# A hybrid encoder layer on one core: another order of three dense products, before and inside retention

## The chip, the core and the metric

The kernel runs on one core of a Trainium2 chip. A core has a matrix engine (TensorE, PE in the profile, whose weight loads are listed as PEld), a vector engine (VectorE, DVE), an activation engine (ScalarE, ACT), a general engine (GpSimd, POOL) and SyncE (SP), which here issues nearly all DMAs. Each engine works through its own queue of instructions in order. TensorE writes its results to the memory PSUM; here ScalarE or VectorE copies them out ("evicts" them), and a PSUM buffer is used again only after that. The metric is device time in microseconds (us) of one execution, as a median over runs.

## What is computed

One encoder layer is applied to a prompt of 1024 rows and a sample of 256 rows with the same weights, which the kernel handles as 1280 tokens, ten blocks of 128. Cut to what matters:

```python
proj = rms_norm(h, norm_g) @ w_in
(a_qkv, a_gate, a_beta, a_alpha, b_q, b_k, b_v, b_gate, c_q, c_k, c_v, c_gate) = split(proj)
# a: gated delta rule, forward and backward, 6 heads of 64
o_a = rms_norm(delta(q, k, v, beta, g) + flip(delta(flipped))) * silu(a_gate)
# b: retention, forward and backward, 6 heads of 64
o_b = head_layer_norm(retention(bq, bk, bv) + flip(retention(flipped))) * silu(b_gate)
# c: windowed attention with sink and ALiBi, 4 query heads, 2 key heads
o_c = window_attention(cq, ck, cv, sink) * silu(c_gate)
h = h + concat(o_a, o_b, o_c) @ w_out
h = h + (p @ w_ple) * sigmoid(h @ w_pg)
return rms_norm(h, final_g)
```

Inside a chunk of 64 tokens the delta rule needs the inverse of a triangular 64 x 64 matrix; between chunks a 64 x 64 state is passed on. All numbers are 32-bit floats.

## The kernel before

**Dense products.** The projection is cut into products of 128 columns for all 1280 tokens. For near-full precision each 32-bit operand is split into a high and a low part, and a product is the sum of three matmuls (high-high, low-high, high-low) over eight slices of the inner dimension. `dense` runs over token blocks of 512, 512 and 256; each block is 24 matmuls into one PSUM buffer with the tag `mm`, which has two. So two finished blocks can wait for their eviction, and a third cannot start. The weights of the next product are loaded (`raw`) and split (`whi`, `wlo`) one product ahead by `dense_stream`.

The products have short names. Numbers are gates: 0, 1 and 2 are the gates of the delta rule's three pairs of heads, 3 to 5 those of retention's three pairs, 6 and 7 those of attention. `cq0`, `cq1`, `ck`, `cv` are attention's queries, keys and values. `q0` to `q2`, `k0` to `k2`, `v0` to `v2` are retention's, one for each pair of heads. In the order rows and the trace they all read `mm<-xh,whi`; a number behind `mm` is one block, a number behind `whi` one product.

**Evictions.** A `q`, `k` or `v` is evicted by one ScalarE copy per block (L390). A gate takes a copy to `sz` (L468), three activations that make a sigmoid in `sg` (L100 to L102), a VectorE product (L89), and for gates 0 to 5 a DMA to DRAM (`gd`, L472). `sz` and `sg` have one buffer each. Gates 0 to 2 are read back only at the kernel's end, in `fin`; gates 3 to 5 in `av`.

**Where they go.** The region `ot` has eight slots of 1280 columns. k0 and k2 are evicted into slot 0 and every `v` into slot 1; k1 goes to a tile of its own, `kx`. Slots 0 and 1 are also where the triangular inverses are built: `invert` (from L398 on) is a chain of some sixty VectorE operations on these slots, run for two groups of chunks, one after the other. Its end is a memset (L424) and two stores to DRAM (`yd`, L426). The first eviction of k0 must wait until the second group's stores have read slot 0.

**Streams.** Three streams run at once. The *scan* (`scan_stream`) joins the inverses into full ones (`join`: `an`, `yn`, `p1s`, `yc`, tiles in PSUM tag `sb`) and then takes twenty steps forward and backward (`step`: small matmuls into `sa`, state copies `sv` at L729 and L730, the residual `r`, loads of `l`, `yc`, `vt`, `kn`). The *fill* (`fill`) runs attention over ten blocks, with the products of the list `PB` beside it, then retention. For each of the three pairs retention first does `kv(p)` (transposes at L942 and L947, `sb<-bvt,kd`, and a chain of state sums on VectorE at L966) and then `av(p)` (scores `ss`, output, norm). The list `RS` says which products stand beside each of these seven places. The first chain of sums for pair p reads slot 1, so the eviction of the next `v` waits for it.

**What sets the order.** `spread` and `weave` interleave the streams as the program is written, by weights such as `T_AT` and `T_KV`. The framework's scheduler then orders each engine's instructions by an estimate of its own, with evictions at high priority. So two lists of names decide the order only through that scheduler. The rows shown below are what it makes of them.

Of the kernel before, what the change touches and what calls it, by code (L numbers as in the profile page):

```python
# [34 lines left out]
AO = tuple(range(NB))  # L35
X2, SPN = 4, 0
PP = ["cq0", "cq1", 6, 7, 3, "ck", "cv", 4, 0, 5]
PB = [1, 2, "q0"]
RS = [["k0", "v0"], ["q1"], ["k1", "v1"], ["k2"], ["v2"], ["q2"], []]
T_PREP = 10.0  # L40
YB, VB, KB, QB = 1, 2, 1, 1
QLB = 1
# [11 lines left out]
def encoder_kernel(ctx: ExitStack, tc: tile.TileContext, I, O, dbg=None, upto=99):  # L54
# [385 lines left out]
    def spread(*run):  # L440

        run = [[0.0, t, g] for t, g in run]
        while run:
            q = min(run, key=lambda e: e[0])
            t = next(q[2], None)
            if t is None:
                run.remove(q)
            else:
                q[0] += t / q[1]
                yield t  # L450

    def length(ns):
        return 12.8 * len(ns) or 1.0, prods(*ns)
# [31 lines left out]

    PSEQ = PP + PB + [n for r in RS for n in r]

    def prods(*names):
        for n in names:
            i = PSEQ.index(n)  # L490
            yield from dense_stream(n, PSEQ[i + 1] if i + 1 < len(PSEQ) else None)
# [588 lines left out]
    def fill():  # L1080
        nonlocal av
        yield from spread((10 * T_AT, attn_stream()), length(PB))
        cb_cm.__exit__(None, None, None)
        rc_cm, rt_cm, *r = ret_open()
        kv, av = ret_streams(*r)
        yield from prods(*RS[0])
        for p in range(3):
            yield from spread((13 * T_KV, kv(p)), length(RS[1 + 2 * p]))
            if p < 2:
                yield from spread((5 * T_AV, av(p)), length(RS[2 + 2 * p]))  # L1090

        raw = [a[:, 0:4 * GW].rearrange("p (k c) -> p k c", k=4) for a in (kreg[1], ot[:, 1, :])]
        for i in range(2):
            nc.sync.dma_start(out=raw[i], in_=I["w_out"][0][512 * i:512 * i + 512, 0:GW].rearrange("(k p) c -> p k c", p=128))
        yield from spread((5 * T_AV, av(2)), length(RS[6]))

# [120 lines left out]
```

## Time and profile before

| | |
|---|---|
| median of 3 runs | 1095.5 us (1093.81 to 1100.48) |
| the profiled execution | 1098.55 us |
| its span, first to last instruction | 1096.7 us |
| mean granted TensorE clock | 0.959 |
| attention (first scores to the last output) | about 350 to 598 us |
| second inversion ends on VectorE | 463.45 us |
| retention's three pairs of keys start at | 598.8, about 702 and 776.1 us |

Times in the trace count from the span's start. In the rows of the timeline a line gives the start, the duration, the engine, the source line, the operation, what it writes and reads, the shapes and the count; a bracket at its end gives the idle time of that engine before it and what ended it. In a row of windows the stretch is followed by its length and by the busy time of PE, PEld, VectorE, ScalarE and GpSimd, each with a count, then the granted TensorE clock, the share of DMA time and GB/s. A row of the chain of waits has a start, a duration and what the end of the program was waiting for. Matmul rows overlap, because matmuls are pipelined: the pace is the distance of their starts. A matmul of two 32-bit operands that are not split shows as two in the trace (12 for a row of 6 in the order).

### The profile page before, as it was taken

Reading aid. Unit: us, or ns where it says so; the run is one execution under the profiler, and the core shown is the slowest. Engines: PE = TensorE matmul, PEld = TensorE weight load, DVE = VectorE, ACT = ScalarE, POOL = GpSimd, SP = SyncE. Lnnn points to the kernel's source line nnn. Section 1 sums busy time; section 2 is a strip of 40 time slices with the busy share of each in tenths; the row PEclk is TensorE's granted clock in tenths of the full one; section 3 lists DMA queues with packets and bytes.
Section 4 is the critical chain, followed back from the end, with each engine's and each line's share of the span. In section 5 each row is a group of like instructions: output and inputs, shape, how many; then the busy total and the mean of one; then the engine's idle time right before and its main releaser. Section 6 shows DMA issues by size and latency. Waiting matters only on the chain.

```text
span 1096.7 us, 23201 instructions
## 1 busy us (share of the span) xinstructions
PE 1023.4 (93%) x8909; PEld 868.3 (79%) x8909; DVE 640.9 (58%) x1371; ACT 521.8 (48%) x1265; POOL 271.3 (25%) x430
## 2 busy tenths in 40 slices
PE   5999999999897889999998899999799999999996
PEld 4768878887775767878776777777579999999996
DVE  6666677477799679845565755575883123311125
ACT  7576776577456445344444322323342013455554
POOL 2001000022123021222233325544442211233421
PEclk9999999999999889999999799969889999999999
DMA  8112112367866363463464334554372432101003
GB/s 259 35 44 68 44 39 61 75 169 199 194 176 186 84 159 86 111 136 86 111 167 120 108 92 122 138 152 115 112 244 86 144 112 78 39 1 49 11 39 154
DMA packets 201415, 120.70 MB, mean 110 GB/s; under 512 B 105042, under 2 KB 186234, under 8 KB 201306
## 3 DMA queue, kind: packets, MB, share of 16 engines
q1 hardware_dynamic: 196410, 118.97, 39.8%
q8 instruction: 70, 1.15, 0.4%
q0 software_dynamic: 4896, 0.27, 0.4%
q14 instruction: 39, 0.32, 0.1%
HBM read 76.26 MB, written 42.91 MB: 109 GB/s over the span
## 4 chain that ended last, share of the span: by engine, by line
PE 63%; DVE 14%; DMA 10%; issue 4%; ACT 3%; SPq 2%; POOL 2%; DVEq 0%; ACTq 0%; POOLq 0%
PE mm L86 36%; PE sa L86 14%; PE sb L86 6%; PE tr L86 3%; DMA ad<-at 3%; DVE ot L89 3%; DVE l L89 1%; DMA yd<-ot 1%; SPq L618 1%; DMA gd<-sg 1%; DVE ot L966 1%; DMA vt<-vtd 1%; DMA yn<-yd 1%; DMA xt<-in_x_prompt 1%; PE tr L848 1%
## 5 line engine op out<-in xcount | busy, mean ns | idle before, releaser
L86 PE MATMUL mm<-xh,whi 128*128 128x512 f32 x720 | 270.0, 375 | 13.9 <-ACT sz L468 11.5
L86 PE MATMUL mm<-xl,whi 128*128 128x512 f32 x720 | 265.3, 369 | 0.0
L86 PE MATMUL mm<-xh,wlo 128*128 128x512 f32 x720 | 264.2, 367 | 0.0
L86 PEld LDWEIGHTS mm<-xh,whi 128*128 128x128 f32 x720 | 139.5, 194 | 40.0 <-ACT sz L468 13.5
L86 PEld LDWEIGHTS mm<-xh,wlo 128*128 128x128 f32 x720 | 139.6, 194 | 21.6 <-issue 0.5
L86 PEld LDWEIGHTS mm<-xl,whi 128*128 128x128 f32 x720 | 140.1, 195 | 20.5 <-issue 0.7
L89 DVE TENSOR_TENSOR ot<-ot 128x1284 f32<-128x1284 f32 (+16 forms) x131 | 88.0, 672 | 20.0 <-ACT ot L102 15.1
L86 PE MATMUL sa<-whi,xh 128*128 128x256 f32 x320 | 91.1, 285 | 0.0
L86 PE MATMUL sa<-whi,xl 128*128 128x256 f32 x320 | 90.4, 282 | 0.4 <-DVE xl L89 0.4
L86 PE MATMUL mm<-whi,xh 128*128 128x256 f32 x320 | 90.7, 284 | 0.0
L86 PE MATMUL mm<-whi,xl 128*128 128x256 f32 x320 | 90.4, 283 | 0.1
L86 PE MATMUL mm<-wlo,xh 128*128 128x256 f32 x320 | 90.3, 282 | 0.0
L86 PE MATMUL sa<-wlo,xh 128*128 128x256 f32 x320 | 90.1, 281 | 0.0
L89 DVE TENSOR_TENSOR sgm<-sb,sgm 128x256 f32<-128x256 f32 x40 | 17.0, 424 | 94.0 <-ACT sgm L102 73.8
L86 PEld LDWEIGHTS sa<-whi,xl 128*128 128x128 f32 x320 | 60.2, 188 | 0.8 <-DVE xl L89 0.6
L86 PEld LDWEIGHTS mm<-whi,xh 128*128 128x128 f32 x320 | 60.4, 189 | 0.4 <-issue 0.2
L86 PEld LDWEIGHTS sa<-whi,xh 128*128 128x128 f32 x320 | 60.2, 188 | 0.5 <-issue 0.3
L86 PEld LDWEIGHTS mm<-whi,xl 128*128 128x128 f32 x320 | 60.2, 188 | 0.5 <-DVE xl L89 0.3
L86 PEld LDWEIGHTS mm<-wlo,xh 128*128 128x128 f32 x320 | 60.3, 188 | 0.2 <-issue 0.2
L86 PEld LDWEIGHTS sa<-wlo,xh 128*128 128x128 f32 x320 | 60.2, 188 | 0.0
L525 DVE SCALAR_TENSOR_TENSOR ot<-ot,cols 128x1284 f32<-128x1284 f32 x36 | 55.9, 1552 | 0.6
L86 PE MATMUL sa<-sv,l 128*64 128x64 f32 (+1 forms) x912 | 47.3, 240 | 7.8 <-DVE sv L730 4.6
(294 smaller groups left out, 2097.3 us busy)
## 6 DMA issues: line engine op xcount, KB each, us to landing
raw<-in_w_in SPq DMA_DIRECT2D x28, 512.0 KB, 3.8
l2d<-l SPq DMA_DIRECT2D x20, 576.0 KB, 3.6
l<-l2d SPq DMA_DIRECT2D x40, 288.0 KB, 3.2
xt<-in_x_prompt SPq DMA_DIRECT2D x8, 512.0 KB, 6.9
x<-in_x_prompt SPq DMA_DIRECT2D x32, 128.0 KB, 2.7
raw<-in_w_pg SPq DMA_DIRECT2D x4, 1024.0 KB
yp<-ot SPq DMA_DIRECT2D x8, 512.0 KB, 2.7
ad<-at SPq DMA_DIRECT2D x20, 198.0 KB, 3.1
```

The costliest lines, as they stand in the source:

```text
L86: nc.tensor.matmul(out, lhsT, rhs, start=start, stop=stop)
L89: eng.tensor_tensor(out=out, in0=a, in1=b, op=op)
L525: V.scalar_tensor_tensor(out=Y[:, 0:1284], in0=R[:, j:j + 1284], scalar=cw(ti, j), in1=Y[:, 0:1284], op0=MUL, op1=ADD)
L618: nc.sync.dma_start(out=AGD[d][b // 5][q, 2 * b % 10:2 * b % 10 + 2].rearrange("c p r x -> r (c p) x"), in_=at[32 * q:32 * q + 32, :, :, q ...
L848: nc.tensor.transpose(pt[:, k * 128:(k + 1) * 128], pr[:, k * 128:(k + 1) * 128], ident)
L966: V.scalar_tensor_tensor(out=st[r, b2, h], in0=st[r, b, h], scalar=gs[r, 2 * p + h:2 * p + h + 1], in1=kvt[r, b, h], op0=MUL, op1=ADD)
```

## The change

Two lists of product names differ, and nothing else:

```diff
-PB = [1, 2, "q0"]
-RS = [["k0", "v0"], ["q1"], ["k1", "v1"], ["k2"], ["v2"], ["q2"], []]
+PB = [1, "q0", "k0"]
+RS = [["v0"], ["q1"], ["k1", "v1"], ["k2", 2], ["v2"], ["q2"], []]
```

Gate 2 leaves its place beside attention and comes behind k2, in the list that stands beside `kv(1)`. q0 and k0 each move up by one product; k0 is now in attention's own list. The products run in the order 1, 2, q0, k0, v0, q1, k1, v1, k2, v2, q2 before, and 1, q0, k0, v0, q1, k1, v1, k2, 2, v2, q2 after. Every instruction is there in both. Three places show what the scheduler makes of it.

TensorE while attention's third block computes its scores (`sb<-kst,qh`) and the scan its first step. Before, where `mm_5892` is q0's last block and `mm_6112` is k0's first:

```order
L86 MATMUL mm_5892<-xh,wlo_4632 128x256
L86 MATMUL mm_5892<-xh,whi_4631 128x256
L86 MATMUL mm_5892<-xl,whi_4631 128x256
L86 MATMUL mm_5892<-xh,wlo_4632 128x256
L86 MATMUL mm_6112<-xh,whi_5340 128x512
L86 MATMUL mm_6112<-xl,whi_5340 128x512
L86 MATMUL sa_4556<-sv_4557,l_543_4549 64x64 x6
L86 MATMUL sa_4596<-sv_4597,l_550_4589 64x64 x6
L86 MATMUL sb_4291<-kst_3724,qh_4263 128x384
L86 MATMUL sb_4291<-kst_3724,qlz_3753 128x384
```

The same place now, up to the same scores `sb_4291`:

```order
L86 MATMUL sb_4284<-kst_3724,qh_4263 128x384
L86 MATMUL sb_4284<-kst_3724,qlz_3753 128x384
L86 MATMUL sa_4556<-sv_4557,l_543_4549 64x64 x6
L86 MATMUL sa_4596<-sv_4597,l_550_4589 64x64 x6
L86 MATMUL sa_4556<-sv_4560,kn_4754 64x64 x6
L86 MATMUL sb_4291<-kst_3724,qh_4263 128x384
L86 MATMUL sb_4291<-kst_3724,qlz_3753 128x384
```

No dense matmul is left in it. k0's first two blocks now stand ahead of these rows, and its third, which needs one of the two buffers, comes behind the first eviction of k0.

SyncE's queue around the stores of the second inverse (`yd_0`). Before:

```order
L138 DMA raw_6284<-in_w_in 128x8x128
L657 DMA an_4881<-ad_0_397 32x5x32 x6
L713 DMA kn_5540<-knd 128x192
L713 DMA kn_5587<-knd 128x192
L426 DMA yd_0_405<-ot 3840x1x32
L426 DMA yd_0_407<-ot 3840x1x32
```

And now:

```order
L697 DMA yc_5517<-ycd_1_410 128x192
L713 DMA kn_5522<-knd 128x192
L697 DMA yc_5564<-ycd_1_412 128x192
L699 DMA vt_5566<-vtd_415 128x192
L713 DMA kn_5569<-knd 128x192
L699 DMA vt_5717<-vtd_416 128x192
L687 DMA ycd_1_410<-yc_4425 128x5x192
L699 DMA vt_5753<-vtd_415 128x192
L426 DMA yd_0_405<-ot 3840x1x32
L426 DMA yd_0_407<-ot 3840x1x32
```

The stores now stand behind the loads of the scan's third step (`yc_5517`, `yc_5564`, which need the buffer of the second step) and behind the write of the fourth join (`ycd<-yc_4425`).

TensorE in retention's second pair, `kv(1)`, whose keys are `kx`. Before:

```order
L86 MATMUL sb_7887<-bvt_7715,kd_7885 64x64 x4
L947 MATMUL tr_7903<-ident,kx 128x128
L86 MATMUL sb_7897<-bvt_7715,kd_7895 64x64 x4
L947 MATMUL tr_8022<-ident,kx 128x128
L86 MATMUL sa_4596<-sv_7844,kn_7993 64x64 x6
L86 MATMUL sa_4556<-r_7954,yc_7941 64x64 x6
L86 MATMUL sb_7907<-bvt_7715,kd_7905 64x64 x4
L947 MATMUL tr_8032<-ident,kx 128x128
```

And now, where `mm_8075` is gate 2's last block and `mm_8301` is v2's first:

```order
L86 MATMUL sb_7709<-bvt_7516,kd_7707 64x64 x4
L947 MATMUL tr_7909<-ident,kx 128x128
L86 MATMUL mm_8075<-xl,whi_7525 128x256
L86 MATMUL mm_8075<-xh,wlo_7526 128x256
L86 MATMUL mm_8075<-xh,whi_7525 128x256
L86 MATMUL mm_8075<-xl,whi_7525 128x256
L86 MATMUL mm_8075<-xh,wlo_7526 128x256
L86 MATMUL mm_8301<-xh,whi_7872 128x512
L86 MATMUL mm_8301<-xl,whi_7872 128x512
```

Before, v2's first two blocks had been computed beside `av(0)` and waited in PSUM. Now gate 2's first block and most of its second take that place, and the end of gate 2 and v2's first two blocks stand between the small matmuls of `kv(1)`, up to v2's third block.

## The prediction

> **What bounds the kernel now.** I read the page's busy lines, clock slices and chain first, then the stretches by window, then each engine's timeline around the two places between which the work moves.
>
> ```profile
> PE 1023.4 (93%) x8909; PEld 868.3 (79%) x8909; DVE 640.9 (58%) x1371; ACT 521.8 (48%) x1265; POOL 271.3 (25%) x430
> PEclk9999999999999889999999799969889999999999
> PE 63%; DVE 14%; DMA 10%; issue 4%; ACT 3%; SPq 2%; POOL 2%; DVEq 0%; ACTq 0%; POOLq 0%
> ```
>
> TensorE is the bound as a whole, but the dips of its clock mark stretches where it runs out of work. The change adds and drops no TensorE work, so it can only open or fill such dips. The stretches (PE, PEld, DVE, ACT, POOL busy; granted clock; DMA):
>
> ```profile
> 425.00:450.00 25.00, 25.00 (x283) 20.06 (x281) 22.44 (x45) 9.40 (x20) 3.27 (x4) 0.96 0.45 112
> 438.00:468.00 30.00, 30.00 (x436) 23.93 (x435) 24.33 (x64) 9.04 (x23) 7.30 (x10) 1.00 0.49 111
> 475.00:500.00 25.00, 25.00 (x296) 19.78 (x296) 17.07 (x55) 11.62 (x32) 7.55 (x13) 1.00 0.45 115
> 525.00:550.00 25.00, 25.00 (x375) 19.79 (x374) 13.37 (x37) 12.14 (x30) 6.67 (x11) 1.00 0.53 125
> 550.00:575.00 25.00, 23.15 (x394) 18.39 (x392) 17.75 (x59) 10.60 (x31) 8.04 (x14) 1.00 0.62 162
> 575.00:600.00 25.00, 23.32 (x293) 17.08 (x292) 14.26 (x59) 9.88 (x34) 7.93 (x22) 1.00 0.42 109
> 600.00:612.00 12.00, 5.58 (x88) 4.58 (x84) 8.01 (x30) 7.79 (x27) 8.15 (x23) 0.69 0.38 105
> 700.00:730.00 30.00, 28.49 (x366) 22.10 (x358) 22.34 (x69) 9.57 (x31) 15.00 (x25) 0.73 0.58 165
> ```
>
> Attention with the second inversion (to about 468 us) has VectorE and TensorE both full. From 475 to 550 TensorE alone is full. Retention's second pair of keys (704 to 730) has no dense product and a clock of 0.73: that is a dip worth filling.
>
> One dependency decides the first place. The keys k0 are evicted (L390) into the region in which the inversion works, so their first eviction waits for the inversion's result to reach DRAM:
>
> ```profile
> 463.45 0.11 DVE L424 MEMSET ot<- 120x64 f32 x1
> 463.59 6.05 DMA yd<-ot
> 469.72 0.59 ACT L390 COPY ot<-mm 128x512 f32<-128x512 f32 x1 [6.21 <-DMA yd<-ot]
> ```
>
> VectorE ends the inversion at 463.45, the store lands after 6.05, ScalarE has stood for 6.21. Two PSUM buffers hold dense results, so no product can pass its third block while k0's first is not evicted.
>
> **The change part by part.** A block of 512 is 24 matmuls; these are the first and the last of one, and the first and the fourteenth of a 256 block:
>
> ```profile
> 368.59 0.40 PE L86 MATMUL mm<-xh,whi 128*128 128x512 f32 x1
> 373.95 0.40 PE L86 MATMUL mm<-xh,wlo 128*128 128x512 f32 x1
> 374.18 0.28 PE L86 MATMUL mm<-xh,whi 128*128 128x256 f32 x1
> 375.72 0.28 PE L86 MATMUL mm<-xl,whi 128*128 128x256 f32 x1
> ```
>
> That is 5.36/23 = 0.233 us a matmul, 5.6 us a block, and 1.54/13 = 0.118, 2.8 us a small block: 14.0 us for a product.
>
> *At attention.* Gate 2's 14.0 us go, q0 and k0 move up by one place. By the order k0's second block now ends where q0's second ended, at about 438 us. Up to the eviction at 469.72 TensorE had 13.8 us of dense work (9 + 14 matmuls at 0.233, 24 at 0.233, 24 at 0.118); now it has none. So the 30 us row above loses 13.8 and keeps 16.2 of attention, joins and scan: the change opens a hole.
>
> How soon the hole closes is VectorE's matter. The durations:
>
> ```profile
> 422.52 0.69 DVE L89 TENSOR_TENSOR sg<-sg,sz 128x512 f32<-128x512 f32 x1
> 435.90 0.41 DVE L89 TENSOR_TENSOR sg<-sg,sz 128x256 f32<-128x256 f32 x1
> 424.48 1.19 DVE L89 TENSOR_TENSOR wlo<-raw,whi 128x1024 fp32r<-128x1024 f32 x1
> 471.92 0.35 DVE L730 COPY sv<-sa 64x192 f32<-64x192 f32 x1 [4.48 <-ACT sv L729]
> 462.37 0.36 DVE L89 TENSOR_TENSOR r<-sa,bed 128x192 f32<-128x192 f32 x1
> ```
>
> Ahead of the inversion's end its queue loses gate 2's three products and one weight split (0.69 + 0.69 + 0.41 + 1.19 = 3.0) and gains two state copies and one residual (1.1): 1.9 earlier. But matmuls in a hole run at half clock (below), and the inversion's steps stand in VectorE's queue behind results of them. 16.2 us of small matmuls would take 0.84/0.53 times as long, 9.5 us more. If none of that is in VectorE's way, and the 3.4 us that its timeline shows it waiting between 415 and 452 go too, the end is 5.3 earlier; if all is, 7.6 later. I take 0: the 1.9 eaten by as much delay. On SyncE's queue the store now stands behind a read that waits for the scan's step and behind the fourth join's write. By VectorE's order both are ready before the inversion's last row, so at some 0.5 us per issue they add about 1 us at most, inside those ends.
>
> At the eviction more is behind us than before: k0's second block is finished (10 matmuls, 2.3 us), and by the order three more score pairs and 48 scan matmuls are done, three transposes fewer:
>
> ```profile
> 475.61 0.71 PE sb L86 x4
> 488.18 0.84 PE sa L86 x24
> 524.59 0.81 PE tr L848 x6
> ```
>
> 6 × 0.71/4 + 2 × 0.84 - 0.4 = 2.4, with the 2.3 a lead of 4.7 us. It holds through 475 to 550, where TensorE is full. Against it stands the clock. At 350 to 366 this program shows what a hole costs:
>
> ```profile
> 355.54 0.80 PE L86 MATMUL sb<-kst,qlz 128*128 128x256 f32 x2 [5.10 <-DVE qlz L89]
> 359.70 0.79 PE L86 MATMUL mm<-xh,whi 128*128 128x512 f32 x1 [3.36 <-ACT sz L468]
> 365.41 0.55 PE L86 MATMUL mm<-xl,whi 128*128 128x512 f32 x1
> 365.80 0.39 PE L86 MATMUL mm<-xh,wlo 128*128 128x512 f32 x1
> ```
>
> After waits of 5.10 and 3.36, dense matmuls ran at half pace from 359.70 to 365.80: 6.1 us for 3.1 us of work, so +3.0 (ends 0 and 3.0). [...]
>
> Attention's last three blocks come about 27 dense matmuls earlier in the queue, which can fill waits of 1.85 + 1.68 in the rows 550 to 600. I take half, -1.7 (0 to -3.5). Behind it retention's tables and kx's eviction are the same chain. The 12 us row at 600 stays.
>
> *At retention.* By the order, gate 2's blocks take the seats of v2's first two beside the first pair's output, so there nothing is added, and its third block with v2's first two slides into the keys of the second pair: 2.8 + 5.6 + 5.6 = 14.0 us more dense work between its first transposes and v2's third block. What does that stretch absorb?
>
> ```profile
> 707.28 0.56 PE L86 MATMUL sa<-sv,kn 64*64 64x64 f32 x12
> 707.81 0.57 PE L86 MATMUL sa<-sv,l 128*64 128x64 f32 x12
> 711.55 0.45 PE L86 MATMUL sb<-bvt,kd 128*64 128x64 f32 x8 [1.26 <-ACT sab L1019]
> 712.00:716.00 4.00, 3.75 (x52) 2.78 (x51) 3.90 (x15) 1.11 (x4) 0.62 (x1) 0.74 0.76 224
> 718.17 0.91 PE L86 MATMUL sa<-sv,l 128*64 128x64 f32 x12
> 719.01 0.91 PE L86 MATMUL sa<-sv,kn 64*64 64x64 f32 x12
> 724.00:728.00 4.00, 4.00 (x36) 2.93 (x32) 2.94 (x9) 0.58 (x2) 1.89 (x2) 0.50 0.36 112
> 728.00:732.00 4.00, 4.00 (x40) 3.60 (x39) 3.86 (x13) 1.35 (x4) 1.99 (x4) 0.63 0.42 115
> ```
>
> It waited 1.26 + 0.25, then 714 to 731 ran at 0.50: 2.1 us of the row at 712, 12 to 728, 3.0 after it, 17.1 in all. Twelve scan matmuls take 0.84 there (718.17 to 719.01) and 0.53 at full clock (707.28 to 707.81). Filled with dense work the clock has no reason to fall, so 17.1 × 0.31/0.84 = 6.3 come back, and with the waits 7.8. Gate 2 costs 14.0 - 7.8 = +6.2 (ends: +3 if the scan's chain bounds the stretch and hides more, +14 if nothing is absorbed).
>
> Gate 2's eviction is a copy, three activations and a store in place of a copy. I cost it at nothing: ScalarE is busy 9.57 of 30 there. If that cover is gone, the cost is ScalarE standing, since the next block's first activation waits for the store of the one before (one buffer), with the scan's state copies (L729) queued behind it.
>
> The sum: 0 - 4.7 + 3.0 - 1.7 + 6.2 = +2.8 us on the profiled execution's 1098.55, so 1101.35. That execution lies 3.05 above the median of the runs, so 1098.3 there, taken as 1098.
>
> **The rivals.** *Slower: ScalarE blocked by the gate's single buffer.* In attention the worst such wait was
>
> ```profile
> 413.66 0.42 ACT L100 ACTIVATE sg<-sz 128x256 f32<-128x256 f32 x1 [4.49 <-DMA gd<-sg]
> ```
>
> and there ScalarE had slack. In the scan's stretch the store shares SyncE's queue with reads that wait for buffers. Two such waits (second and third block) are 9.0, hence +11.8: about 1107. It decides from 4 us a wait on. Against it: the scan's steps leave ScalarE several waits of 1 to 2 us of their own. Chance 0.16. *Slower: the hole holds up the inversion,* all 9.5 of it, +10.4, 1106. It decides once TensorE's half-pace work fills the whole 30 us; 25.7 fits, which speaks against. Chance 0.14.
>
> *Faster: the hole costs nothing and the second keys absorb more.* VectorE 5.3 earlier, no cold restart, waits 3.5 filled, +3 at retention: -5.3 - 4.7 - 3.5 + 3 = -10.5, 1085. It needs every term at its end. Chance 0.12.
>
> *The change does not do what it says:* by the order the gate itself runs beside the first pair's output and v2 beside the second keys. The work that fills is the same, so this changes no time; and k0 is computed at attention's end but cannot be evicted sooner. If instead the gain and loss cancel to nothing, 1095 to 1096: inside my case.
>
> **How the numbers follow.** My case (the terms near their middles, 1090 to 1104) has 0.58, the rivals 0.16, 0.14 and 0.12. The range: low end 1087, just short of the fast rival's 1085, high end 1110, the blocked ScalarE's 1107 with the inversion partly late; it leaves out about 2 in 10. One per cent, about what a measurement of this kernel can tell from no change, is 11 us: 1084.5 and 1106.5. Faster than that takes all of the fast rival and some: 0.1. Slower is most of the first slow rival and half of the second, 0.22. The rest, 0.68, is within.
>
> **What would show it.** Right: TensorE waits and a clock near 0.5 between 440 and 468; the first k0 eviction still released by the inversion's store, within 3 us of 469.7; a lead of 1 to 5 us near 550; a clock near 1.0 in the second keys and that stretch longer by 4 to 8. Wrong: an inversion that ends 5 us off, a clock that stays up in the hole, or waits of L100 for the gate's store above 3 us in retention.

## The result and the profile after

| | before | after |
|---|---|---|
| median | 1095.8 us (8 runs, 1093.6 to 1100.5) | 1103.0 us (8 runs, 1099.8 to 1105.9) |
| ratio | 1 | 1.006, 95% interval 1.0041 to 1.0079 |
| the profiled execution | 1098.55 us, span 1096.7 | 1103.22 us, span 1100.6 |

The change costs 7.2 us by the medians and 3.9 us between the two profiled spans. It lies inside the range of the prediction (1087 to 1110), 5 us above its 1098.

The page's busy lines, clock slices and chain for the kernel after, in the same places as those of before:

```profile
PE 1026.9 (93%) x8909; PEld 865.9 (79%) x8909; DVE 642.1 (58%) x1371; ACT 522.0 (47%) x1265; POOL 272.0 (25%) x430
PEclk9999999999999989689999899999879999999999
PE 70%; DVE 12%; DMA 9%; issue 3%; ACT 2%; SPq 2%; POOL 1%; DVEq 0%; ACTq 0%; POOLq 0%
```

A slice is about 27.5 us. The dip of 6 that stood in the slice from 713 us is gone (9 now) and the 7 in the one from 603 is an 8. There is a new 6 in the slice from 440, with an 8 behind it, and the 8 in the one from 796 is a 7. The same stretches as before, by window:

```profile
438.00:468.00 30.00, 25.25 (x389) 19.30 (x389) 22.83 (x70) 12.10 (x33) 9.95 (x18) 0.72 0.64 138
475.00:500.00 25.00, 23.92 (x263) 18.16 (x264) 14.73 (x43) 9.66 (x25) 4.47 (x9) 0.86 0.32 75
600.00:612.00 12.00, 7.73 (x81) 6.97 (x78) 7.09 (x23) 6.95 (x21) 6.88 (x17) 0.57 0.46 118
700.00:730.00 30.00, 30.00 (x360) 23.52 (x361) 23.06 (x65) 11.44 (x32) 10.79 (x17) 1.00 0.48 135
```

Both sides of the trade are there. The second keys (700 to 730) are full at clock 1.00, where they had 0.73. Attention's middle (438 to 468), full at 1.00 before, now works 25.25 of 30 us at 0.72. The inversion's end, the issue of its stores on SyncE and k0's first eviction, from the timeline:

```profile
457.37 0.11 DVE L424 MEMSET ot<- 120x64 f32 x1
...
459.07 5.58 SPq L426 DMA_DIRECT2D yd<-ot  x2
...
465.71 1.07 ACT L390 COPY ot<-mm 128x512 f32<-128x512 f32 x2 [3.27 <-DMA yd<-ot]
```

The inversion ends 6.1 us earlier, the eviction 4.0 us: the stores left SyncE 1.7 us after the inversion's end and released it 6.6 after they were issued.

One profiled execution starts its stages a little earlier or later than another, so I measure stages from one row that the change leaves alone, the copy of gate 0's first block (L468, at 345.55 us before and 345.09 after). Each kernel was profiled twice (the repeats are the first two experiments):

| from gate 0's first copy, us | before | before, again | after | after, again |
|---|---|---|---|---|
| inversion's end (L424) | 117.9 | 118.2 | 112.3 | 113.4 |
| k0's first eviction | 124.2 | 124.9 | 120.6 | 121.9 |
| kx's first eviction | 266.2 | 268.2 | 262.3 | 263.2 |
| second keys, first transposes (L942) | 355.8 | 356.4 | 348.9 | 350.1 |
| third keys, last row of L942 | 430.5 | 431.6 | 431.4 | 432.6 |
| end of the span | 751.1 | 752.6 | 755.5 | 758.1 |

All differences here are first profile against first and repeat against repeat; the two profiles of one kernel differ by up to 2.6 us. The lead grows to 6.3 to 6.9 us at the second keys. The stretch from the second to the third keys takes 7.3 to 7.9 us more and eats it. Then 3.4 to 4.5 us are lost behind the third keys (320.6 and 321.0 before, 324.1 and 325.5 after). Those three make 4.4 to 5.5 us. The median's 7.2 is more, since both profiled executions of before (1098.55 and 1097.76) lie 2 to 3 us above its median and those of after (1103.22 and 1102.69) at theirs: 2 to 3 us of the difference are in no profile pair.

### The profile page after: what moved, and what is told of

Same layout as the page of the kernel before. It is cut to its first block, busy times and chain, and to the rows that moved or that the text cites. A ratio compares the mean times of both kernels' runs of the same rounds, so it can differ in the third digit from the quotient of the medians.

```text
span 1100.6 us, 23199 instructions
## 1 busy us (share of the span) xinstructions
PE 1026.9 (93%) x8909; PEld 865.9 (79%) x8909; DVE 642.1 (58%) x1371; ACT 522.0 (47%) x1265; POOL 272.0 (25%) x430
## 3 DMA queue, kind: packets, MB, share of 16 engines
q8 instruction: 70, 1.15, 0.4%
## 4 chain that ended last, share of the span: by engine, by line
PE 70%; DVE 12%; DMA 9%; issue 3%; ACT 2%; SPq 2%; POOL 1%; DVEq 0%; ACTq 0%; POOLq 0%
PE mm L86 40%; PE sa L86 16%; PE sb L86 7%; PE tr L86 4%; DVE ot L89 3%; DVE l L89 2%; DMA yd<-ot 1%; DMA ad<-at 1%; DMA yn<-yd 1%; DMA gd<-sg 1%; SPq L618 1%; PE tr L848 1%; DMA xt<-in_x_prompt 1%; DVE at L89 1%; PE tr L1159 1%
## 5 line engine op out<-in xcount | busy, mean ns | idle before, releaser
L86 PE MATMUL sa<-wlo,xh 128*128 128x256 f32 x320 | 90.1, 281 | 0.0
```

Of the source, the lines that this page charges most:

```text
L86: nc.tensor.matmul(out, lhsT, rhs, start=start, stop=stop)
```

## The experiments

Edits are shown against the kernel that each paragraph names. Ratios are to the kernel before, run beside it on the same chip; the chips differ between experiments, so ratios compare better than times.

### The two profiles again

No edit.

> The kernel before, once more, for how much one profiled execution differs from another. From the two profiles so far: from the start of the second pair's keys to the start of the third's 74.7 us before and 82.6 after; from the last copy of the scan's output on ScalarE (L745) to the end 320.2 and 320.0; from the third pair's keys to the end 320.6 and 324.1. If these are the kernel's own, this profile gives 74.7 within 1.5, 320.2 within 1.5 and 320.6 within 1.5. If they are chance, it is off by 3 or more in one of them.

> The changed kernel, once more. If the differences are the kernel's own: 82.6 within 1.5 us between the starts of the second and third pair's keys, 320.0 within 1.5 from the scan's last output copy to the end, and 324.1 within 1.5 from the third pair's keys to the end. If the last 3.5 us are chance, the last figure is near 320.6 here.

Measured: 75.2 and 82.5 between the second and third keys, 320.6 and 320.8 from the scan's last output copy to the end, 321.0 and 325.5 from the third keys to the end. All lie within their bounds, the last one just. So the loss behind the third keys belongs to the changed kernel.

### Each half of the change alone

Against the kernel before, k0 alone joins attention's list; and gate 2 alone moves:

```diff
-PB = [1, 2, "q0"]
-RS = [["k0", "v0"], ["q1"], ["k1", "v1"], ["k2"], ...]
+PB = [1, 2, "q0", "k0"]
+RS = [["v0"], ["q1"], ["k1", "v1"], ["k2"], ...]
...
+PB = [1, "q0"]
+RS = [["k0", "v0"], ["q1"], ["k1", "v1"], ["k2", 2], ...]
```

> Gate 2 stays in attention's list, k0 joins it: the products run in the order they had before, only the pacing of k0 changes. My theory (the time goes where gate 2 is taken out and put in, not where k0's name stands): 1096, between 1093 and 1099; the second inversion ends within 3 us of 463.5, the first k0 eviction within 3 us of 469.7, the second pair's keys keep a granted clock near 0.73. Rival (k0 at attention's end is what costs): 1099 or more, with k0's first eviction no earlier and a TensorE that waits behind k0's second block before it.

> Gate 2 goes to the second pair's keys, k0 stays in retention's first list: the products run in the order of the changed kernel. My theory: the same as the changed kernel, 1103 within 2 us; the second inversion ends within 3 us of 457.4, TensorE runs at a clock near 0.5 between 440 and 465, the lead at the second pair's keys is 6 to 9 us and is gone by the third pair's keys (start near 776.5). Rival (the cost is k0's place): 1096 within 2 us.

k0 alone: 1095.1 us, 0.9997 (0.9982 to 1.0012). The inversion's end (459.87) and k0's eviction (466.15) lie 0.6 us outside their bounds, in an execution that was 1.9 us ahead of before's at gate 0 already; the clock from 700 to 730 was 0.83 where I had expected 0.73. Gate 2 alone: 1100.0 us, 1.0053 (1.0032 to 1.0073); inversion's end at 457.12, the lead gone at the third keys (430.4 us behind gate 0's copy, before 430.5). At the second keys the lead was 10.5 us where I had expected 6 to 9, and the stretch to the third keys took 85.1 us, 10.4 more than before. By the ratios (1.0053 alone, 1.006 with k0's move) gate 2's move carries the cost, and k0's name in the list costs nothing that can be told. The time was 1 us below the bounds that I had set, and the profiled execution, 1097.5, was the fastest of its six; the last experiment returns to it.

### Gate 2 at three other places

Against the kernel after: as the last product; ahead of k1; back in attention but behind k0.

```diff
-PB = [1, "q0", "k0"]
-RS = [["v0"], ["q1"], ["k1", "v1"], ["k2", 2], ["v2"], ["q2"], []]
+RS = [["v0"], ["q1"], ["k1", "v1"], ["k2"], ["v2"], ["q2"], [2]]
...
+RS = [["v0"], ["q1"], [2, "k1", "v1"], ["k2"], ["v2"], ["q2"], []]
...
+PB = [1, "q0", "k0", 2]
+RS = [["v0"], ["q1"], ["k1", "v1"], ["k2"], ["v2"], ["q2"], []]
```

> The changed kernel, but with gate 2 as the very last product, behind q2. My theory (gate 2 costs its 14 us less what the place absorbs, and the stretch ahead of the third pair's keys is full: TensorE 44.9 of 46 at full clock): the second pair's keys go back to a clock near 0.73 and are 8 us shorter, the third pair's keys start some 6 us later than in the changed kernel, near 782.5, and the time is near 1109, at least 1105. Rival (the end of retention is bound by VectorE and the scan, so that dense work there is hidden): third pair's keys within 2 us of 776.5, time at most 1101.

> The changed kernel, but with gate 2 ahead of k1, beside the first pair's output. My theory (what counts is the room at the place): between 575 and 612 the changed kernel's TensorE stood 8.1 us and worked at 0.57 in the last 12, some 3.3 us lost, so up to 11.4 of gate 2's 14 are absorbed: kx is first evicted within 4 us of 607, the second pair's keys take 8 us less than in the changed kernel, and the time is 1098 to 1101. Rival (gate 2 costs about 8 us anywhere in retention): 1103 within 1.5 us. If the tail's loss behind 776 comes from the seat of the scan's last steps alone, it shows here too as some 3 us from the start of the third pair's keys to the end more than before.

> The changed kernel with gate 2 back in attention's list, but behind k0, so that it can't fill the stretch in which k0 waits for the inversion. Theory H (what costs is the hole: 14 us of dense work taken out of it save only the 3.5 to 4.5 us by which k0 is evicted earlier, and must be done where TensorE is full): the first k0 eviction within 3 us of 465.5, TensorE at half clock between 450 and 465, the first pair's keys at 604 to 609 in place of 595, the second pair's keys to the third's 75 within 2, time 1105 to 1109. Theory K (the cost is gate 2 in the second pair's keys, and attention has room for it): time 1095 to 1098.

*Last:* 1109.4 us, 1.0125 (1.0107 to 1.0143), third keys at 783.0, as my theory said; the clock from 700 to 730 fell again, though only to 0.89. Second to third keys take 90.1 us, 15.4 more than before: where TensorE is full (44.92 of 46 us busy at clock 1.00 from 730 to 776 in the kernel after), gate 2 cost its 14 us and a little.

*Ahead of k1:* 1108.5 us, 1.012 (1.0101 to 1.0138), where I had expected 1098 to 1101. This experiment's windows, and who released kx's first eviction, show why:

```profile
575.00:600.00 25.00, 25.00 (x235) 18.69 (x235) 15.83 (x54) 12.73 (x37) 4.54 (x10) 1.00 0.36 99
600.00:612.00 12.00, 11.73 (x141) 8.43 (x139) 4.29 (x17) 3.14 (x10) 3.87 (x14) 1.00 0.42 110
612.00:650.00 38.00, 33.11 (x361) 26.27 (x363) 23.11 (x66) 14.70 (x46) 12.94 (x30) 0.82 0.42 112
```

```profile
623.16 1.07 ACT L390 COPY kx<-mm 128x512 f32<-128x512 f32 x2 [1.91 <-DVE wret L904]
```

The hole at 600 was filled, and opened again behind 612. It waits for retention's tables (`wret`), which come after attention, and gate 2, queued ahead of attention's last rows on TensorE, put those off: kx was evicted at 623.2 in place of 607.4. A hole that moves with the work queued behind the filler can't be filled from ahead. The expectation's last clause is answered too: from the third keys to the end it took 321.6 us, near before's 320.6 and 321.0, so the tail's loss does not show here; the scan's last copy stood 0.4 us behind the third keys, as before.

*Behind k0:* 1108.9 us, 1.0114 (1.0084 to 1.0145), as theory H said, with the eviction at 468.45, the first keys at 603.4 (0.6 us earlier than its bounds) and 75.8 us between the second and third keys. The half clock that I expected of its hole did not come (0.89 from 450 to 466, at 12.31 of 16 us busy), and it cost as much. So the cost of the hole is here the work left undone in it, and not its half clock.

### The scan as the bound

In four profiles (before and after, the repeats) the end followed the scan's last output copy by 320.0 to 320.8 us. Two edits to the kernel after tested whether that copy sets the end:

```diff
-T_JOIN, T_AT, OF, HV = 5.0, 5.4, 6, ()
+T_JOIN, T_AT, OF, HV = 5.0, 5.4, 6, (); T_STEP = 9.0
...
+T_JOIN, T_AT, OF, HV = 5.0, 5.4, 6, (); T_LEAD = 0.0
```

The values so far were 10 for a step's weight and -10 for the place in time at which the fill starts against the scan.

> The changed kernel, with the weight of a scan step at 9 in place of 10, so that the scan's steps stand earlier in the program; by the order of rows the scan's last product on TensorE then stands ahead of the third pair's keys (before: ahead too; changed kernel: behind). Dense products and gate 2 stay as in the changed kernel. Theory A (the scan's end, then its norms and the reads for the output product, set the end; the changed kernel lost in the scan's last steps): the scan's last output copy comes 2 to 4 us earlier against the third pair's keys, the end is again about 320 behind that copy, the time is 1099 to 1101. Theory B (retention's dense work sets the end, the scan has slack): 1103 within 1.5.

> The changed kernel, with the fill started 10 units later against the scan, so that the scan is further ahead everywhere: by the order 450 of its 912 products are done at the first pair's keys in place of 390, and its last one stands 15 rows ahead of the third pair's keys. Theory A (the scan's end sets the end): time 1097 to 1100, the scan's last output copy at least 4 us ahead of the changed kernel's. Theory B (dense work and retention's chain set the end): 1103 within 1.5, or slower, since what the scan takes earlier retention gets later.

A scan step's weight of 9: 1102.9 us, 1.0064 (1.0042 to 1.0086). The copy came 2 us earlier (778.3), but the third keys 3.6 to 4.7 us later (780.2), and the end followed the copy by 324.4 us. The scan ahead everywhere: 1131.7 us, 1.0328 (1.0302 to 1.0354); kx's first eviction moved to 633.4, 26 us later, and the end followed the copy by about 330. So 320 us behind the copy is no rule: theory A as a rule of its own falls.

### The last read of l

In the tail the trace of after shows TensorE standing for a read of the scan, in the timeline of SyncE, TensorE and ScalarE:

```profile
775.90 0.40 SPq L695 DMA_DIRECT2D l<-l2d  x1
...
780.01 0.57 PE L86 MATMUL sa<-sv,l 128*64 128x64 f32 x12 [1.54 <-DMA l<-l2d]
...
780.62 0.32 ACT L745 COPY os<-sa 128x192 f32<-128x192 f32 x1 [2.08 <-PE sa L86]
```

In before the same products needed no wait and the copy came at 776.47:

```profile
771.65 0.55 SPq L695 DMA_DIRECT2D l<-l2d  x1
...
775.56 0.57 PE L86 MATMUL sa<-sv,l 128*64 128x64 f32 x12
...
776.47 0.31 ACT L745 COPY os<-sa 128x192 f32<-128x192 f32 x1
```

The edit, made to the kernel after, to the first experiment's, and to the second's:

```diff
-        nc.sync.dma_start(out=l2, in_=L2D[d][c // 2][c % 2])
+        (nc.gpsimd if last else nc.sync).dma_start(out=l2, in_=L2D[d][c // 2][c % 2])
```

> The changed kernel, with the reads of l for the steps that end a run of the scan issued by GpSimd in place of SyncE; by the order of rows TensorE is the same up to the scan's last products. In two profiles of the changed kernel SyncE issued the last of these reads at 775.9 and 774.9, behind the stores of the scan's outputs, 4 us later than before, and the scan's last output copy came at 780.6 and 780.2, the end 320.0 and 320.8 behind it. Theory A (that queue is where the tail's 3.5 to 4.5 us come from): the last copy within 1.5 us of 777, the stretch from the third pair's keys to the end back to 321 within 1.5, the time 1098.5 to 1100.5. Theory B (retention's own chain sets the end in the changed kernel too, the late scan is hidden): the copy comes earlier, the time stays at 1103 within 1.5.

> The kernel before with k0 in attention's list (the first experiment, 1095.1) and the last reads of l issued by GpSimd. There the scan's last output copy and the third pair's keys were both 320.1 to 320.2 ahead of the end. If both chains bind, one of them made shorter gains nothing: 1095 within 1.5. If the scan's tail alone sets the end: 1092 or less.

> The kernel of the second experiment (gate 2 moved, k0 in retention's list, 1100.0) with the last reads of l issued by GpSimd. In its profile the scan's last output copy came 3.3 us behind the third pair's keys (0.4 before, 4.1 and 4.7 in the changed kernel), yet from those keys to the end it took 321.0 us, as before. Theory A (a late last copy costs its lateness): 1097 within 1 us, copy within 1.5 us of the third pair's keys. Theory C (a late copy costs only with the changed kernel's order of rows behind it, so there is nothing to gain here): 1100 within 1.5 us.

*To the kernel after:* 1099.3 us, 1.0037 (1.0017 to 1.0057), 3.6 us better by the medians, though the intervals of the two ratios overlap (1.0041 to 1.0079 without the edit). The wait is gone from the row of the last products, and the copy follows the third keys by 1.4 us in place of 4.1:

```profile
778.48 0.88 PE L942 MATMUL tr<-ident,ot 128*128 128x128 f32 x6
779.28 0.57 PE L86 MATMUL sa<-sv,l 128*64 128x64 f32 x12
...
779.92 0.34 ACT L745 COPY os<-sa 128x192 f32<-128x192 f32 x1
```

From the third keys to the end it is 321.0 us, as theory A said (the copy's own time was 1.4 us past its bound, in an execution that was 2 us later at the third keys already).

Where in the tail the time goes can be read 30 to 40 us behind the third keys. There the output product (`mm<-wlo,xh` and its like, 128 x 256), which reads the scan's outputs transposed at L1032, goes over to a dense run. The window and the first row of that run, before:

```profile
806.06:816.06 10.00, 9.88 (x75) 7.89 (x73) 9.96 (x18) 4.83 (x11) 2.94 (x4) 1.00 0.86 267
...
805.95 0.41 PE L86 MATMUL mm<-wlo,xh 128*128 128x256 f32 x1
```

In the kernel after:

```profile
806.54:816.54 10.00, 8.23 (x38) 6.33 (x39) 9.31 (x14) 4.30 (x9) 5.46 (x4) 0.50 0.78 232
...
814.50 0.58 PE L86 MATMUL mm<-wlo,xh 128*128 128x256 f32 x1
```

With the edit:

```profile
808.48:818.48 10.00, 9.48 (x74) 7.61 (x72) 9.70 (x17) 5.29 (x11) 3.77 (x6) 1.00 0.75 236
...
808.67 0.38 PE L86 MATMUL mm<-wlo,xh 128*128 128x256 f32 x1
```

The run starts 29.9 us behind the third keys before, 38.0 after and 30.2 with the edit; until then TensorE does small products, at a granted clock of 0.66 before (776.10 to 806.00), 0.71 after (776.50 to 814.50) and 0.75 with the edit (776 to 806). But the edit does more than move a read: the scheduler also puts the scores and outputs of one block of retention less ahead of that row than in the kernel after. So this experiment does not separate the read from the order of rows.

*With k0 in the list:* 1094.7 us, 0.9983 (0.9966 to 0.9999), next to 1095.1 without the edit. So here the edit gains nothing that can be told, as expected of two chains that end together. It is the lowest time of the study, by less than a measurement of this kernel can tell.

*With gate 2 alone moved:* 1105.6 us, 1.0094 (1.0069 to 1.0118), which is neither theory's. Between its profile and that of gate 2 alone lie 8.0 us: 4.6 up to the second keys, 0.3 from there to the third, 3.1 behind. The first part arises where the order of rows on TensorE is the same in both, and it is there at 476 us, before GpSimd issues the first of the moved reads (497.0). The row that restarts TensorE behind k0's first blocks, in the timeline of gate 2 alone:

```profile
474.42 0.56 PE L86 MATMUL sa<-r,yc 64*64 64x64 f32 x12 [1.15 <-DVE r L89]
```

Its window behind that:

```profile
478.00:485.00 7.00, 7.00 (x39) 5.19 (x39) 2.52 (x8) 3.25 (x9) 0.42 (x1) 0.87 0.35 90
```

The same two in the kernel with the edit:

```profile
476.33 1.49 PE L86 MATMUL sa<-r,yc 64*64 64x64 f32 x18 [2.84 <-DVE r L89]
```

And its window:

```profile
478.00:485.00 7.00, 7.00 (x25) 5.31 (x25) 3.98 (x12) 3.90 (x9) 1.01 (x2) 0.50 0.22 53
```

A wait of 2.84 against 1.15 us, and then half clock to 485 against 480. So part of the low profile of gate 2 alone is the luck of one execution. The tails go against theory A from both sides. Gate 2 alone had its copy 3.4 us behind the third keys, and, as in the kernel after, one block more ahead of the output product's dense run, yet its tail took 321.2 us. With the edit the copy is only 1.6 us behind and no block more stands ahead of the run, yet the tail takes 324.2 us. Here TensorE waited for VectorE just ahead of the run, which starts at 811.98, 32.4 us behind the third keys:

```profile
811.42 0.90 PE L1032 MATMUL sa<-ident,oo 128*128 128x128 f32 x3 [3.36 <-DVE gt L1033]
```

Neither a late copy nor that order alone sets the tail. The place of the loss is shown, its cause stays open.

## Why the prediction was near, and where it was off

Point by point, with the terms as the prediction put them:

- **The inversion's end, 0 (ends -5.3 to +7.6):** mis-sized. It came 4.8 to 5.6 us earlier by the table, right at the favourable end; an inversion 5 us off stood among the prediction's own signs of being wrong. The half clock in TensorE's hole (0.50 from 449.10 to 464.20) did not hold VectorE up. VectorE's own windows from 400 us to the inversion's end, before and then after (busy time, clock, DMA share, GB/s):

```profile
400.00:463.50 63.50, 58.69 (x127) 0.97 0.46 114
```

And of after:

```profile
400.00:457.40 57.40, 54.78 (x125) 0.92 0.44 105
```

  That is 3.9 us less work where I had counted 1.9, and 2.2 less waiting where I had let waiting grow.
- **The lead at k0's eviction and the cold restart, -4.7 + 3.0; the tail of attention, -1.7:** the eviction was still released by the store, but 1.0 us outside the 3 us of 469.7 that I had allowed, since it came with the inversion. The restart at 466.35 was at full clock (1.00 from 466.35 to 472.00), which I had wrong. The 3.0 was read from one restart of one execution: at the same place the kernel after shows 3.4 us at half pace in place of 6.1 (rows in the last section). The penalty came at a second wait, for the last join's read of the inverse, which stands on SyncE behind the same stores. VectorE, then TensorE, in the timeline of after:

```profile
473.98 0.68 DVE L664 STREAM_TRANSPOSE xn<-yn 128x480 f32<-128x480 f32 x1 [4.41 <-DMA yn<-yd]
...
476.08 1.49 PE L86 MATMUL sa<-r,yc 64*64 64x64 f32 x18 [3.04 <-DVE r L89]
...
480.99 0.63 PE L86 MATMUL mm<-xh,whi 128*128 128x512 f32 x1
481.42 0.63 PE L86 MATMUL mm<-xl,whi 128*128 128x512 f32 x1
481.85 0.46 PE L86 MATMUL mm<-xh,wlo 128*128 128x512 f32 x1
482.15 0.39 PE L86 MATMUL mm<-xh,whi 128*128 128x512 f32 x1
482.38 0.40 PE L86 MATMUL mm<-xl,whi 128*128 128x512 f32 x1
```

  Dense products start 0.43 us apart up to 481.85 and 0.23 from 482.15. The sum of these terms, with the inversion's 0, was -3.4; at kx's first eviction it measured -3.9 to -5.0, at the second keys -6.3 to -6.9. Part of the last figure is only moved: from the second keys on the traces have 179 dense matmuls in place of 107, which is gate 2's 72, but also 36 to 60 matmuls of the scan more.
- **Gate 2 in the second keys, +6.2 (ends +3 to +14):** +7.3 to +7.9. Right in its mechanism, 1 to 2 us too small: the clock of 1.00 came, and about half of the 14 us was absorbed. The scan's moved matmuls may be a part of that. With gate 2 at the other three places the time was 1108.5 to 1109.4.
- **Behind the third keys:** no term. This is the step that failed. I let the sum end at retention's second keys, as if the rest followed rigidly. What it left out was 3.4 to 4.5 us. The scan's last state copy came 1.6 us later against the third keys (L729 at 774.12 and 776.16), its last read was issued 4.3 us later (771.65 and 775.90), and the output product's dense run began 8 to 10 us later against the third keys (29.9 and 29.6 us behind them before, 38.0 and 40.1 after). With that read elsewhere the kernel after measures 1099.3, but the order of rows moved with it, so which of the two it was is not shown.
- **The rival of a blocked ScalarE** had no part. The three first activations of gate 2 (L100) show no wait for the store; here the second and third:

```profile
700.52 0.63 ACT L100 ACTIVATE sg<-sz 128x512 f32<-128x512 f32 x1
...
709.11 0.40 ACT L100 ACTIVATE sg<-sz 128x256 f32<-128x256 f32 x1
```

- **The rival of a late inversion** gave 1106, near the time measured, by a mechanism that did not happen.

So the clock in the second keys rose as forecast (0.73 to 1.00). But gate 2 made that stretch 7 to 8 us longer, and 14 us of dense work taken from in front of k0 made the second keys only 6 to 7 us earlier. That the forecast came within 5 us is in part luck: on the way to the second keys the sum was about 3 us too pessimistic, and that pays for most of the term it left out.

## What to carry to other kernels

Moving work into a dip of the clock is a trade of two dips: ask what the work covered where it stood, and measure both places from rows of their own. Before filling a hole from ahead, ask what the hole waits for: if that stands on the same engine behind the filler, the hole moves along, as it did from 600 to 612 us. And where several streams end together, put a term into the sum for what comes behind them. An edit that moves one read can move the order of rows too: compare the order before the gain is put down to the read.

## What the runs showed of the hardware

TensorE stayed at half clock for 15 us while the trace has it busy almost throughout. After a stretch with 1.03 of 4.5 us busy, the hole of after reads, by window:

```profile
444.60:449.10 4.50, 1.03 (x14) 0.64 (x14) 4.50 (x11) 2.11 (x6) 3.37 (x5) 0.86 0.63 110
449.10:464.20 15.10, 14.91 (x204) 11.32 (x204) 10.64 (x38) 4.90 (x13) 2.94 (x6) 0.50 0.68 166
464.20:466.30 2.10, 1.73 (x18) 1.33 (x17) 1.07 (x4) 0.59 (x2) 1.00 (x4) 0.83 0.57 90
```

It was filled with 32 x 32 and 64-row products, transposes and a few attention scores, with no dense product among them. The repeat shows the same (13.88 of 14 us from 450 to 464, clock 0.50). That the products are small does not explain it alone. With gate 2 behind k0 the same kinds of product stand at this place, and among them the clock came back:

```profile
442.00:446.00 4.00, 4.00 (x33) 3.23 (x32) 3.84 (x11) 1.27 (x3) 1.19 (x2) 0.50 0.63 159
...
450.00:453.40 3.40, 2.58 (x87) 2.12 (x84) 3.27 (x9) 1.49 (x6) 1.64 (x4) 1.00 0.37 89
```

The way back was no fixed time here either. At the start of attention the prediction's rows show dense matmuls at half pace for 6.1 us, after waits of 5.10 and 3.36. In the kernel after, behind the same two waits, it was 3.4 us, counted in the same way to the first row of 0.39:

```profile
359.23 0.80 PE L86 MATMUL mm<-xh,whi 128*128 128x512 f32 x1 [3.36 <-ACT sz L468]
...
361.96 0.63 PE L86 MATMUL mm<-xh,whi 128*128 128x512 f32 x1
362.38 0.46 PE L86 MATMUL mm<-xl,whi 128*128 128x512 f32 x1
362.68 0.39 PE L86 MATMUL mm<-xh,wlo 128*128 128x512 f32 x1
```

What decides between the 3.4, the 6.1 and the 15 us was not tried.

The second surprise is that the length of one wait did not tell its cost here. Over the same rows on TensorE, small products first and dense ones behind, waits of 1.15 us (gate 2 alone), 3.04 (the kernel after) and 2.84 (gate 2 alone with the read moved) were followed by full clock 5.6, 6.1 and 9.2 us after TensorE went on.
